# First modulation on column groups of TensorE with its loads in the operands' tiles, and modulation shares moved out of an output projection

## The chip, the cores and the metric

The kernel runs on one core of one Trainium2 chip. The metric is the device time of one execution in microseconds. Three runs of the kernel before took 1596.87 to 1600.23 us, median 1598.62.

## What is computed

Two residual blocks on 256 latent tokens and 256 context tokens of width 1024, in float32. Each block modulates, applies a SwiGLU feed-forward (hidden 2816), modulates, applies a mixer (a short convolution in block 0, grouped-query attention with 8 heads in block 1), modulates, and applies a second feed-forward:

```python
mod  = (silu(c) @ mod_w[i] + mod_b[i]).reshape(3, 3, D)       # shift, scale, gate, three times
modc = (silu(c_ctx) @ mod_w[i] + mod_b[i]).reshape(3, 3, D)
modulate(t, g, shift, scale) = rms(t) * g * (1 + scale) + shift
lat += 0.5 * mod[0, 2]  * swiglu(modulate(lat, g0, mod[0, 0], mod[0, 1]), w13, w2)
cx  += 0.5 * modc[0, 2] * swiglu(modulate(cx, g0, modc[0, 0], modc[0, 1]), w13, w2)
# mixer with mod[1], second feed-forward with mod[2]; in block 1 the context stops after the mixer's keys and values
```

The modulation is a product of one vector (two vectors: c and c_ctx) with a matrix of 1024 x 9216 per block.

## The kernel before, in words

Activations lie transposed: 8 tiles of 128 channels by 512 tokens (latent and context side by side). Every matrix product is done three times (`mm3`, lines 113 to 118): weight and activation are each split into a high part (`wh`, `hh`) and a low part (`wl`, `hl`), and high x high, high x low and low x high are added in PSUM. `split` (lines 91 to 93) makes the high part on ScalarE and the low part on VectorE. Weights arrive in `wr` tiles of 128x2048 (three buffers, `load_raw`, line 88, SP's queue).

The work is written with a tile framework that orders the instructions of each engine by readiness and priority, and sets the waits. A tile is allocated from a pool of a fixed number of buffers; an instruction that needs a new tile waits until an old one is free.

A feed-forward works in three parts of its 22 hidden tiles (8, 7, 7). For each hidden tile it loads W (gate and up halves) and does the products `pg` and `pu`; `w13_post` applies silu and product (`sg`, `gm`) and splits the result (`gh`, `gl`). After each part `project` multiplies by w2 (`py`) and adds into x (`finish`, line 440). In the first feed-forward the first eight hidden tiles are done with 48 plain matmuls of 512 columns each. Other parts of it use sums of quarter blocks of h (T1 to T4, `FirstBlocks.sums`, lines 353 to 373) in order to need fewer products.

The modulation is spread over the kernel. The part that the first norm needs (channels 0 and 1: shift B00 and scale A00) is cut into eight pieces (channel, quarter), which I call shares. `mod_pe` (lines 736 to 755) computes one on TensorE: eight matmuls with `sccol` (128 x 2) as the weights over 256 columns, a copy of the row (line 746), and two small matmuls that turn the row into columns (line 748). `mod_dve` computes one on VectorE instead: a load from `modT` and four units of line 136 (`junk`), each the product of a 128x1024 half with the broadcast vector `scbc` and its sum. All later channels are such units. `tick(n)` says how many units are added to the program at a place, and `mod_ready` adds what is still missing where a channel is needed.

The start follows a hand-written list, `FIRST_STEPS` (lines 34 to 37): W is the load and split of one of the first three weights, P a share on TensorE, D a share on VectorE, S the broadcast of the vectors (`load_sc`), N the norm of a quarter of h (`norm_q`: A00, t, hh, hl, and a raw copy hr for the sums), M the matmuls of one weight with one quarter (12 of 512 columns). So "P11 P10 P00 N0" are three shares and then the first quarter of h. Before it come 36 warming matmuls (`idle`) and the sums of squares (lines 214 to 242: `sq`, `acc`, `ss`, `rs`, `ri`, `ris`). After it, `w13_post` of the three weights, and the sums T1 to T4 in the middle of the next hidden tile.

In block 1, `scores`, `turn` and `mix` work through the heads with `tick(0.5)` in the loop; then `project` with `wo` and 1.2 units a tile, then the last norm (`tail_norm(1, 2, ...)`, which needs channels 6 and 7 of block 1) and the last feed-forward.

Of the kernel before, what the change touches and what calls it, by code (L numbers as in the profile page):

```python
# [9 lines left out]
F32 = mybir.dt.float32  # L10
# [3 lines left out]
ALU = mybir.AluOpType  # L14
# [12 lines left out]
KVH = 2  # L27
EPS = 1e-6
WARM = 36

FIRST_STEPS = (
    "W0 P11 P10 P00 N0 P01 N1 P12 W1 S M00 M10 M01 M11 D02 N2 M02 D13 W2 D03 M12 M20 M21 N3 "
    "M03 M22 M13 M23"
)


# [1 line left out]
def hybrid_kernel(ctx: ExitStack, tc: tile.TileContext, a: dict, out: bass.AP):  # L40
# [13 lines left out]
    def nm(s):  # L54
        uid[0] += 1
        return f"{s}{uid[0]}"
# [4 lines left out]
    def psmall(s="pq"):  # L61
        return pss.tile([P, T2], F32, tag="sm", name=nm(s))
# [15 lines left out]
    nc.vector.memset(ones, 1.0)  # L78
    eps_t = const.tile([P, 1], F32, name="eps_t", tag="eps_t")
    nc.vector.memset(eps_t, EPS)  # L80
# [92 lines left out]
    def tick(n):  # L173

        owed[0] += n
        while (jobs or units) and owed[0] >= 1:
            owed[0] -= 1
            next_unit()
# [44 lines left out]
                else:  # L223
                    accs[s, "last"] = part

    def rms_inv(s, parts):

        pq = psmall("ss")
        for i in range(2):
            for n, t in enumerate(parts):  # L230
                nc.tensor.matmul(
                    pq[:, S + i : S + i + 1], t[:, i * P : i * P + P], ones[:, 0:1],
                    start=(n == 0), stop=(n == len(parts) - 1),
                )
# [5 lines left out]
        nc.vector.reciprocal(ri, rs)  # L240
        for i in range(2):
            nc.tensor.matmul(
                pq[:, i * P : i * P + P], ri[:, i : i + 1].to_broadcast([P, P]), ident,
                start=True, stop=True,
            )
        return pq[:, :S]

    def scaled(s, k, A, ri):
        t = tp.tile([P, S], F32, name=nm("t"), tag="t", bufs=3)
        nc.vector.scalar_tensor_tensor(  # L250
            out=t, in0=x[:, k, s * S : s * S + S], scalar=A[:, k, s : s + 1], in1=ri,
            op0=ALU.mult, op1=ALU.mult,
        )
        return t

    def norm_k(s, k, h, A, B, ri, keep=None):
        hh, hl = pick(h, k, s * S, s * S + S)
        t = scaled(s, k, A, ri)
        b = B[:, k, s : s + 1]
        nc.scalar.activation(out=hh, in_=t, func=AF.Identity, bias=b)  # L260
        nc.vector.scalar_tensor_tensor(
            out=hl, in0=t, scalar=b, in1=hh.bitcast(F32), op0=ALU.add, op1=ALU.subtract
        )
        if keep is not None:
            nc.scalar.activation(out=keep, in_=t, func=AF.Identity, bias=b)

    def hot(s, dt=F32R):
        return hop.tile([P, 1024], dt, name=nm(s), tag="hop")
# [336 lines left out]
    def ffn(l, b, h, tot, gate, tail, gs=(), ev=1.5):  # L605
        gs = list(gs)
        i0 = 0
        for t, n in enumerate(THIRDS):
            between = ()
            if tot == T2:  # L610
# [22 lines left out]
                for i in range(len(gs), n):  # L633
                    if t == 0 and not heads and i in AS_IS[l, b]:
                        w = load_w(a["w13"][l, b, i])
                        pp = psum("pg"), psum("pu")
                        if prev:
                            prev.seven()
                        w13_mm(pp, w, h, range(4), 0, T2)
                        if prev:  # L640
                            gs.append(new_pair("g"))
                            prev.four(gs[-1])
                            prev = None
                        w13_mm(pp, w, h, range(4, KT), 0, T2)
                        gs.append(new_pair("g"))
                        w13_post(pp, gs[-1], 0, T2)
                        if "T1" not in h.t:
                            h.sums()
                        else:
                            tick(5)  # L650
# [61 lines left out]

    h = Plain()
    h32 = {}
    idle = psmall("idle")


    for _ in range(WARM):
        nc.tensor.matmul(idle[:, :P], ones, ones, start=True, stop=True)
    for k in range(KT):  # L720
        square_add(k, 0, T2)
    ris = []
    for s in range(2):
        ris.append(tp.tile([P, S], F32, name=nm("ris"), tag=f"ris{s}", bufs=1))
        nc.scalar.copy(ris[s], rms_inv(s, (accs[s], accs[s, "last"])))
# [7 lines left out]
    def both(t):  # L733
        return t.unsqueeze(2).to_broadcast([P, 2, 2])

    def mod_pe(ch, q):

        raw = load_raw(a["mod0"][ch, q])
        pr = psmall("pr")
        for k in range(KT):  # L740
            nc.tensor.matmul(
                pr[:2, :S], sccol[:, k, :], raw[:, k * S : k * S + S],
                start=(k == 0), stop=(k == KT - 1),
            )
        row = tp.tile([P, S], F32, name=nm("row"), tag="t", bufs=3)
        nc.scalar.copy(row[:2, :], pr[:2, :S])
        for j in range(2):
            nc.tensor.matmul(
                pr[:, S + 2 * j : S + 2 * j + 2], row[:2, j * P : j * P + P], ident[:2, :2],
                start=True, stop=True,  # L750
            )
        k2 = slice(2 * q, 2 * q + 2)
        nc.vector.tensor_tensor(
            out=(A00 if ch else B00)[:, k2, :],
            in0=pr[:, S : S + 4].rearrange("p (k v) -> p k v", v=2),
            in1=both(sb1[:, k2] if ch else modb[:, 0, k2]),
            op=ALU.add,
        )

    def norm_q(q):  # L760
        k2 = slice(2 * q, 2 * q + 2)
        nc.vector.tensor_tensor(
            out=A00[:, k2, :], in0=A00[:, k2, :], in1=both(normg[:, 0, 0, k2]), op=ALU.mult
        )
        for k in range(2 * q, 2 * q + 2):
            for s in range(2):
                if (q, s) not in h32:
                    h32[q, s] = gp.tile([P, T2], F32, name=nm("hr"), tag="gl" if s else "gh")
                norm_k(s, k, h, A00, B00, ris[s], h32[q, s][:, (k % 2) * S : (k % 2) * S + S])

    pps = [(psum("pg"), psum("pu")) for _ in range(3)]

    def mod_dve(ch, q):
        mod_job(0, ch, q)
        if ch:
            k2 = slice(2 * q, 2 * q + 2)
            nc.vector.tensor_scalar(
                out=A00[:, k2, :], in0=modv[0, 1][:, k2, :], scalar1=1.0, scalar2=None,
                op0=ALU.add,
            )  # L780

    ws, gs0 = {}, []

# [5 lines left out]
    def first_w(i):  # L789
# [8 lines left out]

    steps = {
        "P": mod_pe,  # L800
        "D": mod_dve,
        "S": load_sc,
        "W": first_w,
        "N": norm_q,
        "M": lambda i, q: w13_mm(pps[i], ws[i], h, range(2 * q, 2 * q + 2), 0, T2),
    }
    for step in FIRST_STEPS.split():
        steps[step[0]](*(int(c) for c in step[1:]))
# [11 lines left out]


    hn = Plain()
    ffn(0, 0, h, T2, lazy_gate(0, 0), tail_norm(0, 1, hn), gs0)
    h = hn

    zs = []
# [256 lines left out]
    pns, pts = {0: scores(0)}, {}  # L1083
    v_proj(2)
    v_proj(3)
    tick(1)
# [21 lines left out]
def _layout(inp):  # L1108
# [53 lines left out]
    sign = np.where(np.arange(P) % 64 < 32, -1.0, 1.0).astype(np.float32)  # L1162
    d["sinT"] = np.sin(ang).T * sign[:, None]
    d["ident"] = np.eye(P, dtype=np.float32)
    return {k: np.ascontiguousarray(v) for k, v in d.items()}


# [17 lines left out]
```

## Time and profile before

| what | value |
|---|---|
| median of three runs | 1598.62 us |
| profiled execution | 1600.64 us |
| its span, first to last instruction | 1598.9 us |
| mean granted TensorE clock | 0.993 |
| TensorE busy | 1575.3 us |
| VectorE busy | 1317.5 us |
| ScalarE busy | 719.0 us |
| moved from memory | 244.77 MB, 154 GB/s over the span |

PE is TensorE, PEld its weight loads, DVE VectorE, ACT ScalarE, SP the engine whose queue issues most transfers. A row of the timeline has the start in us, the duration, engine, line, operation, output and inputs, shape and count; in brackets the idle time ahead of it and what ended that. A row of the windows has, for a stretch of time, its length and then the busy time of PE, PEld, DVE, ACT and POOL with their instructions in brackets, then the granted clock, the busy share of the DMA engines and GB/s. A matmul's duration reaches past the start of the next, since they are pipelined: its cost in a stream is the distance between starts.

### The profile page before, as it was taken

The page shows a single profiled execution, that of the slowest core. Times are in us where ns is not written, and L with a number is a line of the kernel's source. Part 1 is how long each engine was busy: PE and PEld are TensorE (multiplying, and loading weights), DVE is VectorE, ACT ScalarE, POOL GpSimd, SP SyncE. Part 2 cuts the span into 40 slices and gives each one's busy share as a digit, 9 for nine tenths or more (in the row PEclk, how much of TensorE's full clock was granted, in tenths as well). Part 3 has the DMA queues.
Part 4 walks back from the last instruction along what each step waited for, and adds up shares of the span by engine and source line. Part 5 has one row for each costly group of instructions (what it writes and reads, how often), then busy time and mean ns, then how long its engine had stood idle before and what let it go on. Part 6 is the DMA issues. An engine that isn't in the chain of part 4 may idle for free.

```text
span 1598.9 us, 25657 instructions
## 1 busy us (share of the span) xinstructions
PE 1575.3 (99%) x10590; PEld 1450.4 (91%) x10590; DVE 1317.5 (82%) x2005; ACT 719.0 (45%) x1100; POOL 30.3 (2%) x20
## 2 busy tenths in 40 slices
PE   9999999999999999999999999999999999899999
PEld 5788998998888899989899899889899898899999
DVE  3998788889998879798798899898797789875554
ACT  4622452544322356435345376245255456454443
POOL 0000000000000000000000000000000005100000
PEclk9999999999999999999999999999999999999999
DMA  8555225324555512352342423452432454665452
GB/s 289 195 198 202 103 97 181 106 99 179 181 209 192 181 60 100 139 178 100 126 158 96 169 93 106 154 197 103 166 123 106 181 185 165 210 241 185 168 200 104
DMA packets 38278, 248.79 MB, mean 156 GB/s; under 512 B 5136, under 2 KB 6928, under 8 KB 12304
## 3 DMA queue, kind: packets, MB, share of 16 engines
q1 hardware_dynamic: 35712, 245.38, 43.8%
q10 hardware_dynamic: 2448, 1.76, 0.4%
q8 instruction: 83, 1.36, 0.3%
q14 instruction: 35, 0.29, 0.1%
HBM read 244.77 MB, written 1.05 MB: 154 GB/s over the span
## 4 chain that ended last, share of the span: by engine, by line
PE 90%; DVE 6%; ACT 2%; DMA 1%; issue 1%; POOL 0%; ACTq 0%; DVEq 0%; POOLq 0%
PE py L117 9%; PE py L116 9%; PE py L118 9%; PE p L118 6%; PE p L117 6%; PE p L116 6%; PE q L118 5%; PE q L116 5%; PE q L117 5%; PE pg L116 3%; PE pg L118 2%; DVE junk L136 2%; PE pg L117 2%; PE pu L118 2%; PE pu L117 2%; PE pu L116 2%
## 5 line engine op out<-in xcount | busy, mean ns | idle before, releaser
L92 ACT ACTIVATE wh<-wr 128x1024 fp32r<-128x1024 f32 (+2 forms) x276 | 276.7, 1014 | 371.6 <-PE py L117 118.0
L93 DVE TENSOR_TENSOR wl<-wr,wh 128x1024 fp32r<-128x1024 f32 (+2 forms) x276 | 320.7, 1168 | 90.2 <-ACT wh L92 89.6
L136 DVE CUSTOM_DVE_ANT_0 junk<-wr,scbc,modb 128x1024 bf16<-128x1024 f32 x236 | 302.4, 1281 | 29.5 <-DMA wr<-in_modT 26.8
L116 PE MATMUL py<-gh,wh 128*128 128x512 f32 (+1 forms) x746 | 263.2, 353 | 0.0
L117 PE MATMUL py<-gl,wh 128*128 128x512 f32 (+1 forms) x746 | 262.9, 352 | 0.0
L118 PE MATMUL py<-gh,wl 128*128 128x512 f32 (+1 forms) x746 | 262.9, 352 | 0.0
L118 PEld LDWEIGHTS py<-gh,wl 128*128 128x128 f32 x746 | 141.1, 189 | 19.1
L93 DVE TENSOR_TENSOR wl<-ws,wh 128x1024 fp32r<-128x1024 f32 x108 | 131.8, 1224 | 32.2 <-ACT wh L92 32.0
L116 PEld LDWEIGHTS py<-gh,wh 128*128 128x128 f32 x746 | 141.2, 189 | 18.5
L117 PEld LDWEIGHTS py<-gl,wh 128*128 128x128 f32 x746 | 141.2, 189 | 18.1
L92 ACT ACTIVATE wh<-ws 128x1024 fp32r<-128x1024 f32 x108 | 113.6, 1058 | 71.7 <-PE p L117 38.2
L118 PE MATMUL p<-th,wl 128*128 128x256 f32 x432 | 122.3, 283 | 0.0
L117 PE MATMUL p<-tl,wh 128*128 128x256 f32 x432 | 122.2, 283 | 0.0
L116 PE MATMUL p<-th,wh 128*128 128x256 f32 x432 | 122.2, 283 | 0.0
L440 DVE SCALAR_TENSOR_TENSOR x<-py,G,x 128x256 f32<-128x256 f32 x168 | 74.1, 479 | 24.9 <-PE py L118 24.9
L116 PE MATMUL q<-bh,wh 128*128 128x256 f32 x320 | 90.6, 283 | 0.0
L117 PE MATMUL q<-bl,wh 128*128 128x256 f32 x320 | 90.6, 283 | 0.0
L118 PE MATMUL q<-bh,wl 128*128 128x256 f32 x320 | 90.6, 283 | 0.0
L116 PEld LDWEIGHTS p<-th,wh 128*128 128x128 f32 x432 | 82.9, 192 | 0.3
L117 PEld LDWEIGHTS p<-tl,wh 128*128 128x128 f32 x432 | 82.9, 192 | 0.3
L118 PEld LDWEIGHTS p<-th,wl 128*128 128x128 f32 x432 | 82.9, 192 | 0.0
L116 PE MATMUL pg<-hh,wh 128*128 128x256 f32 (+1 forms) x240 | 75.8, 316 | 4.1 <-ACT hh L260 4.1
(236 smaller groups left out, 4054.6 us busy)
## 6 DMA issues: line engine op xcount, KB each, us to landing
wr<-in_w SPq DMA_DIRECT2D x88, 1024.0 KB, 4.9
wr<-in_modT SPq DMA_DIRECT2D x67, 1024.0 KB, 4.9
wr<-in_w2b SPq DMA_DIRECT2D x32, 896.0 KB, 4.6
wr<-in_w2a SPq DMA_DIRECT2D x16, 1024.0 KB, 5.0
wr<-in_cw_cx SPq DMA_DIRECT2D x8, 1024.0 KB, 4.9
wr<-in_mod SPq DMA_DIRECT2D x5, 1024.0 KB, 4.8
wr<-in_cw_b SPq DMA_DIRECT2D x4, 1024.0 KB, 5.0
wr<-in_cw_out SPq DMA_DIRECT2D x4, 1024.0 KB, 4.9
```

Of the source, the lines that this page charges most:

```text
L92: nc.scalar.activation(out=hi, in_=src, func=AF.Copy)
L93: nc.vector.tensor_tensor(out=lo, in0=src, in1=hi.bitcast(F32), op=ALU.subtract)
L116: nc.tensor.matmul(ps, wh, mh, start=first, stop=False, **kw)
L117: nc.tensor.matmul(ps, wh, ml, start=False, stop=False, **kw)
L118: nc.tensor.matmul(ps, wl, mh, start=False, stop=last, **kw)
L136: nc.vector.tensor_tensor_reduce(out=junk, in0=raw[:, j * D : j * D + D], in1=scbc[:, v, :], scale=1.0, scalar=modb[:, l, col : col + 1], ...
L440: nc.vector.scalar_tensor_tensor(out=x[:, m, s * S : s * S + S], in0=ps[:, o : o + S], scalar=g[:, m, s : s + 1], in1=x[:, m, s * S : s * ...
```

## The change

The list of first steps is rewritten. All eight shares go through TensorE. A share's raw data is loaded as two 128x1024 tiles from the pool of the operands' tiles (`hop`), not as one `wr` tile. `sccol` is widened to 32 columns (two filled, the others zero); the eight matmuls of a share write four groups of 32 partitions (`tile_position`), each group taking two of the eight, and the small matmuls that turn the row also add the four groups, with a constant `rowsum`. The turn is a step of its own (T), so that two shares can be computed ahead of two turns; F is eight filling matmuls; H makes the raw copies of a quarter, formerly inside N. TensorE's order in this stretch is fixed as written (`manual_schedule`); the vectors for VectorE's units are loaded where the scheduler has room (S is last in the list). The sums T1 to T4 come right after the first three weights.

Units: six after the first steps, five in each of the next five hidden tiles, 1.8 instead of 1.5 a tile in the first feed-forward's projections, two instead of one and 0.75 instead of 0.5 in attention, none in the projection with `wo`.

```diff
 FIRST_STEPS = (
-    "W0 P11 P10 P00 N0 P01 N1 P12 W1 S M00 M10 M01 M11 D02 N2 M02 D13 W2 D03 M12 M20 M21 N3 "
-    "M03 M22 M13 M23"
+    "P10 P00 T10 T00 N0 F W0 M00 W1 P11 P01 T11 T01 N1 H0 M10 W2 M01 P12 H1 M11 P02 T12 T02 "
+    "N2 M20 H2 M21 P13 P03 T13 T03 N3 M02 M12 M22 H3 M03 M13 M23 S"
 )
-    sccol = const.tile([P, KT, 2], F32, name="sccol", tag="sccol")
-    nc.scalar.activation(out=sccol, in_=ccol, func=AF.Silu)
+    sccol = const.tile([P, KT, 32], F32, name="sccol", tag="sccol")
+    nc.vector.memset(sccol, 0.0)
+    nc.scalar.activation(out=sccol[:, :, :2], in_=ccol, func=AF.Silu)
+
+    rowsum = cload("rowsum", [P, 2])
...
     def mod_pe(ch, q):
-        raw = load_raw(a["mod0"][ch, q])
-        pr = psmall("pr")
+        raws = []
+        for i in range(2):
+            raws.append(hot("pm", F32))
+            nc.sync.dma_start(raws[i], a["mod0"][ch, q, :, i * 1024 : i * 1024 + 1024])
+        pr = psum("pr") if (ch, q) == (1, 0) else psmall("pr")
         for k in range(KT):
+            g = 32 * (k % 4)
+            o = k % 4 * S
             nc.tensor.matmul(
-                pr[:2, :S], sccol[:, k, :], raw[:, k * S : k * S + S],
-                start=(k == 0), stop=(k == KT - 1),
+                pr[g : g + 32, :S], sccol[:, k, :], raws[k // 4][:, o : o + S],
+                start=(k < 4), stop=(k >= 4), tile_position=(0, g),
             )
-        row = tp.tile([P, S], F32, name=nm("row"), tag="t", bufs=3)
-        nc.scalar.copy(row[:2, :], pr[:2, :S])
+        row = tp.tile([P, T2], F32, name=nm("row"), tag="gm", bufs=3)
+        nc.scalar.copy(row[:, :S], pr[:, :S])
+        rows[ch, q] = pr, row
+
+    def mod_turn(ch, q):
+        pr, row = rows[ch, q]
         for j in range(2):
             nc.tensor.matmul(
-                pr[:, S + 2 * j : S + 2 * j + 2], row[:2, j * P : j * P + P], ident[:2, :2],
+                pr[:, S + 2 * j : S + 2 * j + 2], row[:, j * P : j * P + P], rowsum,
                 start=True, stop=True,
             )
...
+    with tc.manual_schedule(engines={mybir.EngineType.PE}):
+        fill(WARM)
+        sums = [rms_sum(s, (accs[s], accs[s, "last"])) for s in range(2)]
+        for step in FIRST_STEPS.split():
+            if step == "P00":
+                for s in range(2):
+                    ris.append(tp.tile([P, S], F32, name=nm("ris"), tag=f"ris{s}", bufs=1))
+                    nc.scalar.copy(ris[s], rms_all(*sums[s]))
+            steps[step[0]](*(int(c) for c in step[1:]))
...
         w13_post(pps[i], gs0[i], 0, T2)
+    h.sums()
+    tick(6)
...
-    ffn(0, 0, h, T2, lazy_gate(0, 0), tail_norm(0, 1, hn), gs0)
+    ffn(0, 0, h, T2, lazy_gate(0, 0), tail_norm(0, 1, hn), gs0, 1.8)
...
-        tick(0.5)
+        tick(0.75)
...
-        by_pairs("wo"), lambda k, c0, c1: aos[k], KT, lazy_gate(1, 1), tail_norm(1, 2, hn), S, 0, 1.2,
+        by_pairs("wo"), lambda k, c0, c1: aos[k], KT, lazy_gate(1, 1), tail_norm(1, 2, hn), S, 0, 0,
```

More of the change, by code (lines that the diff above doesn't have):

```diff
@@ L254, in scaled, with norm_k @@
         return t
[L256 removed]
+    def norm_k(s, k, h, A, B, ri, t=None):
         hh, hl = pick(h, k, s * S, s * S + S)
[L258 removed]
+        t = scaled(s, k, A, ri, t)
         b = B[:, k, s : s + 1]
@@ L263, in norm_k @@
         )
-        if keep is not None:
-            nc.scalar.activation(out=keep, in_=t, func=AF.Identity, bias=b)
+        return t
     def hot(s, dt=F32R):
@@ L646, in ffn @@
                         w13_post(pp, gs[-1], 0, T2)
[L647 to L650, printed above, removed]
+                        tick(5)
                         continue
@@ L714, in hybrid_kernel, with fill @@
     h32 = {}
-    idle = psmall("idle")
-    for _ in range(WARM):
-        nc.tensor.matmul(idle[:, :P], ones, ones, start=True, stop=True)
+    idle = psum("idle")
+    def fill(n):
+        for _ in range(n):
+            nc.tensor.matmul(idle[:, :P], ones, ones, start=True, stop=True)
     for k in range(KT):
         square_add(k, 0, T2)
[L722 to L725, printed above, removed]
     A00 = const.tile([P, KT, 2], F32, name="A00", tag="A00")
@@ L766, in norm_q, with copy_q, first_mm @@
             for s in range(2):
[L767 to L780, printed above, removed]
+                t = None
+                if k % 2:
+                    t = tp.tile([P, T2], F32, name=nm("t"), tag="sg", bufs=3)[:, :S]
+                ts[k, s] = norm_k(s, k, h, A00, B00, ris[s], t)
+    def copy_q(q):
+        for s in range(2):
+            h32[q, s] = gp.tile([P, T2], F32, name=nm("hr"), tag="gl" if s else "gh")
+            for k in range(2 * q, 2 * q + 2):
+                nc.scalar.activation(
+                    out=h32[q, s][:, (k % 2) * S : (k % 2) * S + S], in_=ts[k, s],
+                    func=AF.Identity, bias=B00[:, k, s : s + 1],
+                )
+    pps = {}
+    ris, ts = [], {}
+    def first_mm(i, q):
+        if q == 0:
+            pps[i] = psum("pg"), psum("pu")
+        w13_mm(pps[i], ws[i], h, range(2 * q, 2 * q + 2), 0, T2)
     ws, gs0 = {}, []
@@ L804, in hybrid_kernel @@
         "N": norm_q,
-        "M": lambda i, q: w13_mm(pps[i], ws[i], h, range(2 * q, 2 * q + 2), 0, T2),
+        "M": first_mm,
     }
-    for step in FIRST_STEPS.split():
-        steps[step[0]](*(int(c) for c in step[1:]))
+    with tc.manual_schedule(engines={mybir.EngineType.PE}):
[3 more added lines that the diff above has]
+            if step == "P00":
+                for s in range(2):
+                    ris.append(tp.tile([P, S], F32, name=nm("ris"), tag=f"ris{s}", bufs=1))
+                    nc.scalar.copy(ris[s], rms_all(*sums[s]))
+            steps[step[0]](*(int(c) for c in step[1:]))
     done[0, 0] = done[0, 1] = 16
@@ L1164, in _layout @@
     d["ident"] = np.eye(P, dtype=np.float32)
+    d["rowsum"] = (np.arange(P)[:, None] % 32 == np.arange(2)).astype(np.float32)
     return {k: np.ascontiguousarray(v) for k, v in d.items()}
```

19 lines of the change are left out of this document (14 added, 5 removed).

## The prediction

> **What bounds the kernel now.** I read the page first (shares of engines, then the chain that ended last), then windows over the first 130 us, then the timeline of each engine there.
>
> ```profile
> span 1598.9 us, 25657 instructions
> ...
> PE 1575.3 (99%) x10590; PEld 1450.4 (91%) x10590; DVE 1317.5 (82%) x2005; ACT 719.0 (45%) x1100; POOL 30.3 (2%) x20
> ...
> PE 90%; DVE 6%; ACT 2%; DMA 1%; issue 1%; POOL 0%; ACTq 0%; DVEq 0%; POOLq 0%
> ```
>
> The chain is 90% TensorE, so an edit pays if it starts the dense stream of matmuls earlier or closes one of its holes. The first projection matmul (py) is my milestone: ahead of it, both kernels have the same 384 matmuls of the gate and up products (eight blocks of 48).
>
> ```profile
> 39.38 0.50 PE L116 MATMUL pg<-hh,wh 128*128 128x512 f32 x1
> 67.76 0.50 PE L116 MATMUL pg<-hh,wh 128*128 128x512 f32 x1 [2.82 <-ACT hh L260]
> 130.46 0.39 PE L116 MATMUL py<-gh,wh 128*128 128x512 f32 x1
> 39.38:64.94 25.56, 25.55 (x113) 20.50 (x112) 24.16 (x48) 13.27 (x26) 0.00 (x0) 1.00 0.60 215
> 67.76:130.46 62.70, 62.70 (x276) 51.90 (x277) 59.42 (x89) 25.42 (x38) 0.00 (x0) 1.00 0.57 201
> ```
>
> The third column of a window row is TensorE. From 67.76 it is full: 62.70/276 = 0.227 us per matmul, 2.72 us for a step M of 12, 10.9 us for a block. The stream starts at 39.38 and loses 2.82 us waiting for h. What fills the time before 39.38 are the shares of the first modulation:
>
> ```profile
> 12.63 0.36 PE L231 MATMUL ss<-ones,sq 128*128 128x1 f32 x2
> 12.87 1.38 PE L242 MATMUL ss<-ident,ri 128*128 128x128 f32 x8
> 16.89 1.44 PE L741 MATMUL pr<-wr,sccol 128*2 128x256 f32 x3 [2.64 <-ACT wh L92]
> 28.02 0.60 PE L748 MATMUL pr<-ident,row 2*128 2x2 f32 x4
> 28.55 3.62 PE L741 MATMUL pr<-wr,sccol 128*2 128x256 f32 x16
> 31.34 0.36 ACT L746 COPY row<-pr 2x256 f32<-2x256 f32 x1 [3.71 <-PE pr L741]
> ```
>
> A share is eight matmuls in 16 passes over 3.62 us: 0.44 us a matmul, 0.22 us a pass. Four and a part of the fifth stand before the first gate matmul, and the first waits behind W0's load.
>
> **The change part by part: the start.** All eight shares now go through TensorE, each with its matmuls spread over four groups of 32 columns; their loads have tiles of their own, and the first two are ahead of W0 in SP's queue. No M waits for more than two shares. Three things could set the new start: transfers, the shares' passes, VectorE.
>
> Transfers:
>
> ```profile
> 0.00:10.00 10.00, 8.97 (x62) 8.97 (x63) 3.83 (x15) 5.14 (x9) 0.19 (x4) 1.00 0.86 274
> 10.00:16.00 6.00, 4.25 (x36) 3.91 (x35) 2.65 (x7) 4.81 (x10) 0.00 (x0) 0.95 0.99 401
> 16.00:22.00 6.00, 5.11 (x13) 1.54 (x14) 1.29 (x2) 0.77 (x2) 0.00 (x0) 0.50 0.78 269
> 34.00:46.00 12.00, 12.00 (x57) 7.34 (x56) 10.11 (x25) 11.54 (x23) 0.00 (x0) 1.00 0.85 316
> ```
>
> 2.74 MB move in the first 10 us; with the queue full, 401 GB/s. A share or a W is 1.05 MB, 2.6 us. Since SP no longer waits for one of three buffers before a share, I keep the queue full and count in its new order: P10 12, P00 14, W0 17, W1 20, P11 22, P01 25, W2 27.5, first half of scbc, P12 31, P02 34, second half, two modT, P13 43, P03 46. At 316 GB/s instead, the 36 us after 10 become 45 and P03 lands at 55.
>
> The shares' price is the open one. No row shows a matmul on a group of columns. From below: four at once, 3.54/4 = 0.9 us a share. From above: none overlap, 3.54 (the row). I take 2.0: the row shows two passes per matmul; the second needs the same columns as the first, so only the second pass of one can run beside the first of the next, which leaves one pass of spacing per matmul, 8 x 0.22 + 0.22. The Trainium skill, TensorE: Matmul & The Clock Gate, Part 3, says that matmuls start and end strictly in program order; that fits this count, and no run here shows it for column groups. The same section gives 2.38 times for three column groups; by that figure a share would cost about 1.5 us and the time would be 2 to 3 us under my forecast.
>
> Other durations:
>
> ```profile
> 1.03 10.28 PE L719 MATMUL idle<-ones 128*128 128x128 f32 x72 [1.03 <-DVE eps_t L80]
> 15.10 0.63 ACT L725 COPY ris<-ss 128x256 f32<-128x256 f32 x2
> 33.00 0.51 ACT L260 ACTIVATE hh<-t,mod 128x256 fp32r<-128x256 f32 x1 [1.30 <-DVE mod L753]
> 41.11 1.14 ACT L92 ACTIVATE wh<-wr 128x512 fp32r<-128x512 f32 x2
> 44.85 1.27 DVE L250 SCALAR_TENSOR_TENSOR t<-x,A,ris 128x256 f32<-128x256 f32 x3
> 43.05 1.89 DVE L93 TENSOR_TENSOR wl<-wr,wh 128x512 fp32r<-128x512 f32 x3
> 49.08 1.28 DVE L136 CUSTOM_DVE_ANT_0 junk<-wr,scbc,modb 128x1024 bf16<-128x1024 f32 x1
> 50.29 0.48 DVE L261 SCALAR_TENSOR_TENSOR hl<-t,mod,hh 128x256 fp32r<-128x256 f32 x1
> 74.66 1.22 DVE L93 TENSOR_TENSOR wl<-wr,wh 128x1024 fp32r<-128x1024 f32 x1
> ```
>
> TensorE in the written order: the sums end at 13.0 (12.63 + 0.36), P10 to 15.0, broadcasts 1.4 to 16.4, P00 to 18.4, row copy and turn 1.0 to 19.4. ScalarE then makes three hh and one raw copy (0.4 each) and two pieces of W0 (0.57 each): M00 starts at 22.4 and ends at 25.7, 0.6 of it waiting for wl. The eight fills (0.29 us each, 2.3) lie in those 3.0 us and cost nothing; if h came sooner they would cost up to 2.3. Then P11, P01 to 29.7, copy and turns 1.0, M10, M01 to 36.1, P12, M11, P02 to 42.8, turns to 43.8, M20, M21 to 49.3, P13, P03 to 53.3, turns to 54.3, and the last six steps (16.3) to 70.7. P03 landed at 46 is hidden behind M21; at 55 it costs 4.
>
> VectorE: N2 follows the turns of 43.8 and ends near 46.4. Its order then has eight units (junk, 1.2 each from one start to the next), three sums of 128x512 (0.6), N3 (3.5): 61.3, just before M03 needs it at 62.5. Eleven pieces for T1 to T4 bring 68.0, and gm, wl, gl, gm, wl of the fourth block 72.1. That block's third matmul needs the last wl; it could run at 71.2, so 0.9 is lost. Milestone: 70.7 + 0.9 + five blocks (54.4) = 126.1, against 130.46: **4.4 us gained**. Behind it VectorE has 31 units (6 and five times 5) to spread over 54 us, but its list for each next block ends 3 us or more before TensorE wants it, so I add nothing.
>
> Moved at no cost, with the cover: the raw copies (H) leave the path of hh and lie on ScalarE beside M steps; three shares' bytes replace those of three modT; rowsum's load takes ScalarE's queue half a microsecond before the silu, while x is still landing; the memset of sccol is over before silu needs it. Fixed order on TensorE: behind a waiting share everything waits, which the sum contains.
>
> **Units moved later on.** Twelve units vanish from VectorE at the start; 6.6 more (22 x 0.3) fall in the first FFN's projections, 8 us of VectorE.
>
> ```profile
> 130.00:175.00 45.00, 45.00 (x204) 37.44 (x203) 36.98 (x57) 12.51 (x14) 0.00 (x0) 1.00 0.47 164
> 175.00:400.00 225.00, 224.80 (x1607) 212.59 (x1607) 189.14 (x277) 106.32 (x162) 0.00 (x0) 1.00 0.36 127
> ```
>
> VectorE (fifth column) has 8 of 45 and 36 of 225 us free: nothing taken, up to 8 if cover failed. In the output projection (wo) the units now stop before its last tiles. Before, they stand on the path:
>
> ```profile
> 1396.66 0.28 PE L118 MATMUL py<-a,wl 128*128 128x256 f32 x1
> 1396.93 1.28 DVE L136 CUSTOM_DVE_ANT_0 junk<-wr,scbc,modb 128x1024 bf16<-128x1024 f32 x1 [1.46 <-DMA wr<-in_modT]
> 1398.48 0.48 DVE L440 SCALAR_TENSOR_TENSOR x<-py,mod,x 128x256 f32<-128x256 f32 x1
> 1399.46 0.38 PE L231 MATMUL ss<-ones,sq 128*128 128x1 f32 x2 [0.46 <-ACT sq L214]
> 1400.71 1.27 DVE L136 CUSTOM_DVE_ANT_0 junk<-wr,scbc,modb 128x1024 bf16<-128x1024 f32 x1
> 1400.85 0.88 PE L242 MATMUL ss<-ident,ri 128*128 128x128 f32 x4 [0.55 <-DVE ri L240]
> ```
>
> VectorE waits for a transfer with the last x and acc behind it. Freed, x starts when py ends (1397.0) instead of 1398.48, so 1.5 us; the second unit delays the norm by 0.2 more beyond 1401.73. **1.7 us gained**; what is late next is the norm's own chain. Attention gets 16 units instead of the 18 that I count in the lists of VectorE's instructions: no cost taken, within a unit or two either way.
>
> **Sum.** 4.4 + 1.7 = 6.1 us. The profiled execution took 1600.64 (its span 1598.9 and 1.7 around it), so 1594.5 by its own time; the median of the three runs is 2.0 below it, so 1592.5 is forecast.
>
> **Rivals.**
> Fully overlapped groups: 0.9 us a share. Then transfers bound: P03 lands at 46, M20 and M21 are over at 44.4, P03 ends at 47 to 48, the M steps at 65.4; VectorE (N2 ends 41.5, plus the same 25.7) holds the fourth block to 67.2, milestone 121.2. Gain 9.3 + 1.7: 1587.6. The Trainium skill, TensorEngine Tiling (Array Packing), Theoretical Speedup, promises up to four times for at most 32 columns; nothing here shows it, and the two passes per matmul in the row speak against it.
>
> Groups do not overlap at all: 3.54 us a share on a TensorE that is the bound. All eight then stand on the path, 8 x 1.54 = 12.3 us more, VectorE's 0.9 hidden: M steps end at 83.0, milestone 137.4, 6.9 later than before, less 1.7: **1603.9, slower**. It decides from 6.1/8 = 0.76 us above my 2.0, that is at 2.8 us a share. For it: the row, and three shares more than before; against: the matmuls have disjoint columns.
>
> The change doesn't start earlier as it says: the granted clock halves again. The row 16 to 22 shows 0.50 after 2.64 us of idle TensorE. With P10 and P00 in such a stretch they cost 4 us more, 2 us gained remain: about 1596.5, same. With P10 landed at 12, TensorE goes from the sums straight into P10, so this is less likely; a slow queue (316 GB/s) ends at the same time.
>
> **Chances.** Forecast 0.45 (1590 to 1595), full overlap 0.25, no overlap 0.18, clock or queue 0.12. A measurement tells about 0.2%, 3.2 us, from no change. Faster by over that: forecast and full overlap, 0.70; within: most of the fourth case, 0.10; slower: no overlap and the rest, 0.20. Range 1585 (full overlap with a little more saved in attention) to 1604 (no overlap).
>
> **What would show it.** The first gate matmul near 22 and the first py near 126; a share's 16 passes within 2 us; TensorE at 54 not waiting for P03's transfer; after the wo projection x starting within 0.3 us of py's end. Wrong if a share takes over 2.8 us, if TensorE sits behind a share whose load is late, or if VectorE's eight units delay N3 past M03.

## The result, and the profile after

The changed kernel took 1595.53 us (median of 17 runs, 1593.18 to 1599.21), the kernel before on the same chips 1598.11 us (median of 17, 1595.08 to 1600.65). The ratio is 0.9984 with a 95% interval of 0.9977 to 0.9991: about 2.6 us faster, a gain that the interval separates from nothing, but within the 0.2% that the prediction called the same. 6.1 us were forecast. The profiled execution of the changed kernel took its median, 1595.53 (span 1593.7 and 1.8 around it); that of the kernel before had taken 1600.64, 2.5 more than its own median here.

The page of the changed kernel: TensorE busy 6.5 us less, VectorE's part of the chain that ended last 4% where it was 6%.

```profile
span 1593.7 us, 25820 instructions
...
PE 1568.8 (98%) x10666; PEld 1449.7 (91%) x10666; DVE 1303.3 (82%) x1984; ACT 721.1 (45%) x1103; POOL 29.4 (2%) x20
...
PE 92%; DVE 4%; ACT 2%; DMA 1%; issue 0%; POOL 0%; ACTq 0%; DVEq 0%; POOLq 0%
```

The timeline of TensorE in the changed kernel's start (start, duration, what, and in brackets the wait ahead of it). L757 is a share's matmul (L741 before), L122 to L124 are the three products of a weight and operand pair (L116 to L118 before):

```profile
17.96 0.64 PE L757 MATMUL pr<-pm,sccol 128*32 128x256 f32 x8 [1.74 <-DMA pm<-in_mod]
...
23.09 0.50 PE L122 MATMUL pg<-hh,wh 128*128 128x512 f32 x1
...
28.31 0.64 PE L757 MATMUL pr<-pm,sccol 128*32 128x256 f32 x8 [0.74 <-DMA pm<-in_mod]
29.49 0.64 PE L757 MATMUL pr<-pm,sccol 128*32 128x256 f32 x8 [0.54 <-DMA pm<-in_mod]
...
37.11 1.07 PE L757 MATMUL pr<-pm,sccol 128*32 128x256 f32 x16
...
42.07 1.22 PE L769 MATMUL pr<-rowsum,row 128*128 128x2 f32 x8
...
48.80 1.93 PE L757 MATMUL pr<-pm,sccol 128*32 128x256 f32 x32
50.66 1.22 PE L769 MATMUL pr<-rowsum,row 128*128 128x2 f32 x8
...
69.77 0.50 PE L122 MATMUL pg<-hh,wh 128*128 128x512 f32 x1 [0.39 <-ACT wh L98]
73.20 0.50 PE L124 MATMUL pg<-hh,wl 128*128 128x512 f32 x1 [2.70 <-DVE wl L99]
...
128.90 0.39 PE L122 MATMUL py<-gh,wh 128*128 128x512 f32 x1
```

The first gate matmul comes 16.3 us earlier than in the kernel before (39.38), the first projection matmul py only 1.6 us earlier (130.46). The same 384 matmuls lie between them, so 14.7 us of the lead are given back on the way. Some 11 of these are the six shares and their turns that now stand behind the first gate matmul (26.4 to 31.1, 37.0 to 38.1, 41.0 to 43.2 and 48.7 to 51.7, with 1.3 us of waits among them); the prediction had them in its sum, and between its 22.4 and its 126.1 the lead shrinks by 12.6. What it had not counted on are the 0.7 us by which the first gate matmul comes later than forecast and 2.1 us behind it. The largest single hole is the last wait: TensorE stands at the fourth gate block for 2.70 us because VectorE has not made the low part of its weights. What VectorE and ScalarE did in the meantime (one timeline of each, put in order of time; L142 is a unit of a later modulation, L774 and L264 are the first steps of the last norm tile, N3):

```profile
46.42 1.27 DVE L142 CUSTOM_DVE_ANT_0 junk<-wr,scbc,modb 128x1024 bf16<-128x1024 f32 x1
...
57.04 0.16 DVE L774 TENSOR_TENSOR A<-pr,sb 128x4 f32<-128x4 f32 x1
...
57.31 1.28 DVE L142 CUSTOM_DVE_ANT_0 junk<-wr,scbc,modb 128x1024 bf16<-128x1024 f32 x1
58.51 1.27 DVE L264 SCALAR_TENSOR_TENSOR t<-x,A,ris 128x256 f32<-128x256 f32 x3
59.03 1.31 ACT L274 ACTIVATE hh<-t,mod 128x256 fp32r<-128x256 f32 x3 [7.80 <-DVE t L264]
...
66.59 2.49 DVE L99 TENSOR_TENSOR tl<-hr,th 128x512 fp32r<-128x512 f32 x4
...
71.93 1.22 DVE L99 TENSOR_TENSOR wl<-wr,wh 128x1024 fp32r<-128x1024 f32 x1
```

The turns that N3 needs are over on TensorE at 51.9. VectorE takes them up at 57.04, behind seven of its eight units, and the eighth still goes ahead of N3's first t. From 46.42 to 73.07 it is never idle for longer than 0.6 us, and the last thing in that row is the weight half that TensorE waits for. The windows of TensorE around the hole (length, busy time, granted clock, share of the DMA engines, GB/s) show what it cost beside the wait itself:

```profile
70.00:72.00 2.00, 0.50 (x2) 1.00 0.00 0
72.00:74.00 2.00, 0.80 (x3) 1.00 0.00 0
74.00:76.00 2.00, 2.00 (x6) 0.52 0.84 250
76.00:78.00 2.00, 2.00 (x7) 0.63 0.65 274
```

Right behind it the granted clock is halved from 74.1 to 77.5: six and seven matmuls fit in 2 us where nine do at full clock, some 1.6 us more. The clock is halved once before, from 19.5 to 22.9, behind the wait for the second half of P00; there it falls on the turns and the filling matmuls. Late in the kernel, in the output projection of the attention, the step that the units had blocked is free (timeline of all engines):

```profile
1392.83 0.28 PE L124 MATMUL py<-a,wl 128*128 128x256 f32 x1
1393.15 0.48 DVE L453 SCALAR_TENSOR_TENSOR x<-py,mod,x 128x256 f32<-128x256 f32 x1 [1.35 <-PE py L124]
```

x is started 0.04 us after the last product's end (1393.11); in the kernel before it was 1.54 us.

### The profile page after: what moved, and what is told of

The parts are those of the page before. It is cut to its first block, busy times and chain, and to the rows that moved or that the text cites. A ratio compares the mean times of both kernels' runs of the same rounds, so it can differ in the third digit from the quotient of the medians.

```text
span 1593.7 us, 25820 instructions
## 1 busy us (share of the span) xinstructions
PE 1568.8 (98%) x10666; PEld 1449.7 (91%) x10666; DVE 1303.3 (82%) x1984; ACT 721.1 (45%) x1103; POOL 29.4 (2%) x20
## 4 chain that ended last, share of the span: by engine, by line
PE 92%; DVE 4%; ACT 2%; DMA 1%; issue 0%; POOL 0%; ACTq 0%; DVEq 0%; POOLq 0%
PE py L123 10%; PE py L122 10%; PE py L124 10%; PE p L124 7%; PE p L123 7%; PE p L122 6%; PE q L122 5%; PE q L124 5%; PE q L123 5%; PE pg L122 2%; PE pg L124 2%; PE pg L123 2%; PE pu L124 2%; PE pu L123 2%; PE pu L122 2%; PE pv L122 1%
## 5 line engine op out<-in xcount | busy, mean ns | idle before, releaser
L142 DVE CUSTOM_DVE_ANT_0 junk<-wr,scbc,modb 128x1024 bf16<-128x1024 f32 x224 | 286.9, 1281 | 31.8 <-DMA wr<-in_modT 29.0
L122 PE MATMUL py<-gh,wh 128*128 128x512 f32 (+1 forms) x746 | 263.3, 353 | 0.0
L124 PE MATMUL py<-gh,wl 128*128 128x512 f32 (+1 forms) x746 | 262.7, 352 | 0.0
L124 PEld LDWEIGHTS py<-gh,wl 128*128 128x128 f32 x746 | 141.1, 189 | 19.0
L122 PEld LDWEIGHTS py<-gh,wh 128*128 128x128 f32 x746 | 141.2, 189 | 18.6
L124 PE MATMUL p<-th,wl 128*128 128x256 f32 x432 | 122.3, 283 | 0.0
L122 PE MATMUL p<-th,wh 128*128 128x256 f32 x432 | 122.2, 283 | 0.0
L453 DVE SCALAR_TENSOR_TENSOR x<-py,G,x 128x256 f32<-128x256 f32 x168 | 73.9, 477 | 23.1 <-PE py L124 23.1
L122 PE MATMUL q<-bh,wh 128*128 128x256 f32 x320 | 90.6, 283 | 0.0
L124 PE MATMUL q<-bh,wl 128*128 128x256 f32 x320 | 90.6, 283 | 0.0
L122 PEld LDWEIGHTS p<-th,wh 128*128 128x128 f32 x432 | 82.9, 192 | 0.3
L124 PEld LDWEIGHTS p<-th,wl 128*128 128x128 f32 x432 | 82.9, 192 | 0.0
L124 PE MATMUL pg<-hh,wl 128*128 128x256 f32 (+1 forms) x240 | 75.5, 315 | 2.8 <-DVE wl L99 2.7
```

Of the source, the lines that this page charges most:

```text
L122: nc.tensor.matmul(ps, wh, mh, start=first, stop=False, **kw)
L124: nc.tensor.matmul(ps, wl, mh, start=False, stop=last, **kw)
L142: nc.vector.tensor_tensor_reduce(out=junk, in0=raw[:, j * D : j * D + D], in1=scbc[:, v, :], scale=1.0, scalar=modb[:, l, col : col + 1], ...
L453: nc.vector.scalar_tensor_tensor(out=x[:, m, s * S : s * S + S], in0=ps[:, o : o + S], scalar=g[:, m, s : s + 1], in1=x[:, m, s * S : s * ...
```

## The experiments

**The theory.** TensorE is no longer what holds the start back. VectorE's list is: its units of later modulations stand ahead of the last norm tile, so the early start ends in a wait, and the wait in a halved clock. **Rivals**: TensorE's fixed list and the transfers it waits for set the start; or the shares themselves are still dear. Besides: what the late part (units moved out of the output projection) is worth.

All profiled executions in one table, us, with the median of 4 to 17 runs. "First gate" and "py" are the starts of the first gate and the first projection matmul, "middle" is the time from that py to the first py of the third group in the second layer's first feed-forward, "rest" from there to the end of the span. Ratios are to the kernel before, with 95% intervals.

| kernel | first gate | py | middle | rest | median | ratio |
|---|---|---|---|---|---|---|
| before | 39.4 | 130.5 | 1103.2 | 365.2 | 1598.11 | |
| changed | 23.1 | 128.9 | 1102.4 | 362.4 | 1595.53 | 0.9984 (0.9977 to 0.9991) |
| a_one_chain | 27.3 | 142.3 | 1101.3 | 362.4 | 1607.11 | 1.0051 (1.0038 to 1.0065) |
| f_groups_in_before | 27.7 | 126.1 | 1102.2 | 363.1 | 1596.02 | 0.9985 (0.9975 to 0.9996) |
| e_units_later | 22.1 | 121.2 | 1108.2 | 362.1 | 1593.43 | 0.9976 (0.9965 to 0.9987) |
| e2_units_spread | 22.0 | 124.5 | 1101.8 | 360.9 | 1587.62 | 0.9928 (0.9915 to 0.9941) |
| c_wo_as_before | 21.6 | 128.8 | 1102.6 | 364.5 | 1596.30 | 0.9994 (0.9983 to 1.0004) |
| d_late_alone | 36.3 | 129.0 | 1103.4 | 362.4 | 1597.42 | 1.0002 (0.9993 to 1.0012) |
| g_groups_and_late | 28.8 | 127.8 | 1103.5 | 362.3 | 1594.90 | 0.9978 (0.9969 to 0.9987) |
| e3_more_fill | 22.1 | 122.7 | 1100.4 | 360.9 | 1587.41 | 0.9934 (0.9920 to 0.9948) |
| e4_m10_first | 22.6 | 123.6 | 1102.1 | 363.3 | 1590.09 | 0.9947 (0.9933 to 0.9961) |
| h_no_fill | 21.6 | 121.5 | 1101.9 | 362.4 | 1588.55 | 0.9939 (0.9926 to 0.9952) |

The columns of times come from one execution each, and they scatter: kernels whose edits differ only behind the first py have it 1.5 us apart (before and d), 1.7 (f and g), 0.1 (changed and c, with first gate matmuls 1.5 apart) and 3.3 (e and e2).

### What a share costs: a_one_chain and f_groups_in_before

a_one_chain is the changed kernel with the groups taken out:

```diff
-            g = 32 * (k % 4)
+            g = 0
...
-                start=(k < 4), stop=(k >= 4), tile_position=(0, g),
+                start=(k == 0), stop=(k == KT - 1),
```

> The changed kernel with each share as one chain of eight products in one group of 32 columns (only rows 0 to 31 copied and added up). Theory (the four groups overlap, 1.07 us a share against 3.5): 16 passes near 3.5 us again, eight shares some 20 us longer, of which the transfers that are waited for hide 3 and the vanished wait for VectorE with its half clock gives back 4.3: first output-projection matmul near 141, whole near 1608, ratio 1.006. Rival (groups do not matter here, passes are cheap in any form): 16 passes near 1.1 us, ratio 0.998 as the changed kernel. Rival by the prediction's 2.0 us a share: 8 us slower than the changed kernel, ratio 1.003.

Measured: 1.0051, first py at 142.28. The timeline of its TensorE:

```profile
20.08 3.64 PE L757 MATMUL pr<-pm,sccol 128*32 128x256 f32 x16
...
63.30 7.09 PE L757 MATMUL pr<-pm,sccol 128*32 128x256 f32 x32
```

The same 16 passes take 3.64 us in one group of columns and 1.07 in four: 3.4 times less. Without the groups the changed kernel would have been slower than the one before. The theory's numbers held (141, 1608). The prediction's 2.0 us a share had this kernel at 1.003; that is outside the interval.

f_groups_in_before is the kernel before with the groups, and nothing else of the change:

```diff
-                pr[:2, :S], sccol[:, k, :], raw[:, k * S : k * S + S],
-                start=(k == 0), stop=(k == KT - 1),
+                pr[g : g + 32, :S], sccol[:, k, :], raw[:, k * S : k * S + S],
+                start=(k < 4), stop=(k >= 4), tile_position=(0, g),
```

> The kernel before with only the four column groups of the modulation's shares (one 256-column product of k 0 to 7 in four groups of 32 columns, rows added up by the turn's second operand); tiles, order and units as before. Theory (a share falls from 3.6 to about 1.1 us, but VectorE's order, whose low weights of the fourth block end at 76, sets the time): first gate matmul up to 10 us earlier than 39.4, first output-projection matmul at most 2.5 earlier than 130.5, ratio 0.998 to 1.000. Rival (TensorE's own work sets the start): the first output-projection matmul 8 us or more earlier, ratio 0.995 or less.

Its TensorE, by the timeline:

```profile
32.13 1.07 PE L745 MATMUL pr<-wr,sccol 128*32 128x256 f32 x16
...
61.99 0.80 PE L119 MATMUL pg<-hh,wh 128*128 128x512 f32 x1 [3.05 <-ACT hh L263]
...
126.05 0.39 PE L119 MATMUL py<-gh,wh 128*128 128x512 f32 x1
```

The first gate matmul is 11.7 us earlier than in the kernel before, the first py 4.4 (2.9 against d_late_alone, which has the same front as the kernel before); the wait for the last norm tile stays (3.05, it was 2.82). Ratio 0.9985: the groups alone bring as much as the whole change. The py gain is over the 2.5 that the theory allowed, by either count, and under the 8 of its rival. The new order of loads and of TensorE added nothing measurable to it as it stood; the next two runs show that the units are in its way.

### Who holds the start: e_units_later and e2_units_spread

e_units_later takes the units out of VectorE's way and gives them back later:

```diff
     h.sums()
-    tick(6)
...
-                        tick(5)
+                        tick(7 if i > 4 else 0)
...
-    ffn(0, 0, h, T2, lazy_gate(0, 0), tail_norm(0, 1, hn), gs0, 1.8)
+    ffn(0, 0, h, T2, lazy_gate(0, 0), tail_norm(0, 1, hn), gs0, 2.25)
```

> The changed kernel with no share of a later modulation issued before the sixth gate block (six after the third block and five after each of the fourth and fifth go; seven after each of the last three instead of five, and 2.25 for 1.8 after each output tile make them up), so that VectorE has no such unit ahead of the last first-norm tile. Theory (VectorE's order eats the early start): the wait of 2.7 us for the fourth block's low weights at 73 and the half clock behind it (about 1.6) go, the first output-projection matmul comes near 125 instead of 128.9, the whole near 1591.5, ratio to the kernel before near 0.996. Rival 1 (the fixed order of TensorE and the late transfers set the start): first output-projection matmul stays at 128.9, whole 1595.5, ratio 0.998. Rival 2 (the next one in line, ScalarE's high weights, takes the wait's place): half of it, near 127 and 1593.5.

Its VectorE and, below the dots, its TensorE:

```profile
50.35 0.48 DVE L264 SCALAR_TENSOR_TENSOR t<-x,A,ris 128x256 f32<-128x256 f32 x1
...
61.72 1.23 DVE L99 TENSOR_TENSOR wl<-wr,wh 128x1024 fp32r<-128x1024 f32 x1 [0.72 <-ACT wh L98]
...
63.46 2.35 DVE L99 TENSOR_TENSOR wl<-wr,wh 128x1024 fp32r<-128x1024 f32 x2
...
69.99 1.28 DVE L142 CUSTOM_DVE_ANT_0 junk<-wr,scbc,modb 128x1024 bf16<-128x1024 f32 x1
...
121.18 0.39 PE L122 MATMUL py<-gh,wh 128*128 128x512 f32 x1
...
278.01 0.39 PE L122 MATMUL q<-th,wh 128*128 128x256 f32 x1 [1.58 <-ACT wh L98]
279.27 0.39 PE L124 MATMUL q<-th,wl 128*128 128x256 f32 x1 [0.53 <-DVE wl L99]
```

N3 starts at 50.35 rather than 58.51, the second half of the fourth block's low weights is there by 65.8 rather than 73.2, and py starts at 121.2, 7.7 us earlier than in the changed kernel and more than the 4 expected; e2_units_spread below, with the same front, has 124.5, so 4.4 to 7.7 us. c_wo_as_before, with the changed kernel's front, has its wait of 2.70 us again, and none of the five kernels without the units has a wait of over 0.5 us there: the rival (TensorE's list and the transfers) is out. Of the 7.7, 1.0 is the first gate matmul's, 2.7 the wait, 1.6 the clock behind it; the rest (2.4) is small gaps: raw tiles (0.5 us of waits for 1.3 behind the first gate matmul), the fourth block's high weights (0.4), and N3's tiles, whose lateness stretches M03 by 1.0. By the two ratios the whole gained only some 1.3 us on the changed kernel, and their intervals overlap. The middle grew by 5.8: with 2.25 units after each output tile the second group's weights came late (the last two rows; 4.7 us more from the second group's first py to the third's), with a half clock behind the wait again (windows of TensorE):

```profile
275.00:280.00 5.00, 2.89 (x22) 1.00 0.03 10
280.00:285.00 5.00, 5.00 (x32) 0.66 0.60 210
```

e2_units_spread puts these ten units where VectorE has room:

```diff
-    ffn(0, 0, h, T2, lazy_gate(0, 0), tail_norm(0, 1, hn), gs0, 2.25)
+    ffn(0, 0, h, T2, lazy_gate(0, 0), tail_norm(0, 1, hn), gs0, 1.8)
...
-    ffn(0, 1, h, T2, lazy_gate(0, 2), tail_norm(1, 0, hn), (), 1.7)
+    ffn(0, 1, h, T2, lazy_gate(0, 2), tail_norm(1, 0, hn), (), 1.9)
...
-    ffn(1, 0, h, T2, lazy_gate(1, 0), tail_norm(1, 1, hn), (), 1.6)
+    ffn(1, 0, h, T2, lazy_gate(1, 0), tail_norm(1, 1, hn), (), 1.8)
```

> As e_units_later, but the ten units that its larger share per output tile put into the first feed-forward's projections go into the next two feed-forwards instead (1.8 after each tile of the first as in the changed kernel, then 1.9 for 1.7 and 1.8 for 1.6). Theory (the 4.6 us that e_units_later lost between its second and third groups of output tiles were VectorE's, from those ten units: waits of 2.4 us for the pair's weights and a clock of 0.96): first output-projection matmul near 121, the third group near 341 instead of 345.8, whole 4.6 us under e_units_later, near 1588.5, ratio to the kernel before near 0.994 to 0.995. Rival (the gain is lost again wherever the ten units go): ratio 0.9976 as e_units_later.

Measured: 1587.62 us, ratio 0.9928 (0.9915 to 0.9941), the middle back at 1101.8. That is a version that beats both kernels: 8 us under the changed one by the medians, 9 by the ratios, with the same work. Its py came only at 124.5, with the front that gave 121.2 in e_units_later. The timeline of TensorE shows the waits in it; the longest, 1.46 us, is in both:

```profile
21.96 0.50 PE L122 MATMUL pg<-hh,wh 128*128 128x512 f32 x1 [1.46 <-ACT wh L98]
...
27.34 0.64 PE L757 MATMUL pr<-pm,sccol 128*32 128x256 f32 x8 [0.73 <-DMA pm<-in_mod]
28.52 0.64 PE L757 MATMUL pr<-pm,sccol 128*32 128x256 f32 x8 [0.54 <-DMA pm<-in_mod]
```

and its windows a half clock behind them that e_units_later does not have, from 29.6 to 36.4, which costs some 3.4 us:

```profile
28.00:30.00 2.00, 1.48 (x14) 0.91 0.97 395
30.00:32.00 2.00, 2.00 (x7) 0.50 1.02 406
...
34.00:36.00 2.00, 2.00 (x6) 0.50 1.04 406
```

### The late part: c_wo_as_before, d_late_alone, g_groups_and_late

c undoes it in the changed kernel, d does it alone, g does it with the groups:

```diff
-    tick(2)
+    tick(1)
...
-        tick(0.75)
+        tick(0.5)
...
-        by_pairs("wo"), lambda k, c0, c1: aos[k], KT, lazy_gate(1, 1), tail_norm(1, 2, hn), S, 0, 0,
+        by_pairs("wo"), lambda k, c0, c1: aos[k], KT, lazy_gate(1, 1), tail_norm(1, 2, hn), S, 0, 1.2,
```

(as in c; the other way round in d and g).

> The changed kernel with the second layer's units as before: one and 0.5 per head in the attention, 1.2 after each tile of the output projection. Theory (the late move is worth what the milestones show, 1.2 in the attention and 1.4 behind the output projection): 2.6 us slower than the changed kernel, near 1598, ratio to the kernel before near 1.000. By the prediction's own term (1.7): 1597.2, ratio 0.9995. Rival (these milestones were only scatter between two executions): 1595.5, ratio 0.998.

> The kernel before with only the late part of the change: two and 0.75 units per head in the attention, none in the output projection. Theory: 2.6 us faster than the kernel before, near 1595.5, ratio 0.9984. By the prediction's term (1.7): ratio 0.9989. Rival (scatter): ratio 1.000.

> The kernel before with the column groups of the shares and the late part of the change, and nothing else of it. Theory (late move worth 2 us by the profiled executions: 362.1 to 362.5 us from the last first-layer-width output tiles to the end with it, 363.1 to 365.2 without): 2 us under f_groups_in_before, near 1594, ratio near 0.9972. Rival (the late move is worth nothing, as d_late_alone's ratio of 1.0002 says): ratio near 0.9985.

By the medians' ratios the late part is worth 1.0 thousandth (c against the changed kernel), 0.7 (g against f) and -0.2 (d against before): 1.6, 1.1 and -0.3 us, each with an interval of some 1.5 to 2.2 us either way. In the profiled executions "rest" is 365.2, 363.1 and 364.5 where the late part is missing (mean 364.3) and 360.9 to 363.3 in the nine where it is there (mean 362.1). So about 2 us by the profiles, and 0 to 2 by the times.

The profiles also say that this is not the step that the prediction freed. In c and f the units stand in the projection as before, and the last x is started 0.12 and 0.14 us after its last product all the same: the stall of 1.54 us is in the one execution of the kernel before and not in these. What goes with "rest" is the granted clock, which comes in half-clock periods of 3.4 us (last section). Apart from the one in which the execution ends, "rest" holds four of them in the kernel before (365.2), three in f, c and e4 (363.1, 364.5, 363.3), two in the changed kernel, a, d, g and h (362.3 to 362.4) and one in e, e2 and e3 (360.9 to 362.1). That the late move makes such periods rarer is not shown.

### The half clock in the front: e3_more_fill, e4_m10_first, h_no_fill

```diff
-FILL = 8
+FILL = 14
```

(e3; h has 0. e4 is e3 with the order "P11 M10 P01" instead of "P11 P01 ... M10".)

> e2_units_spread with 14 fill products ahead of the first gate matmul instead of 8, which run on through the 1.46 us that TensorE waits there for ScalarE's high weights. Theory (the half clock seen in the front, 29.1 to some 36 us in e2_units_spread, 18.9 to 23 in the changed kernel, 23.6 to 27 in c_wo_as_before and not at all in e_units_later, is set off by the gaps ahead of it, which add up to 2.7 us in e2_units_spread): no half clock in the front, first output-projection matmul near 121, 1 to 3 us under e2_units_spread, ratio near 0.992 to 0.991. Rival (the clock falls by itself, whatever the gaps): a half-clock stretch of 3 us or more in the front, ratio 0.9928.

> e3_more_fill with the second gate block's first products ahead of the second shift share, so that they lie in the wait for that share's transfer. Theory (what TensorE waits for the raw tiles, 1.7 us in e2_units_spread, is hidden by 12 matmuls): these waits fall under 0.5 us, first output-projection matmul 1 us earlier than e3_more_fill's, ratio near 0.991. Rival (the second block's weights come later than that share): the wait moves to the weights, ratio as e3_more_fill.

> e2_units_spread without the eight fill products between the first turns and the first gate matmul. Theory (gaps set off the half clock): a gap of some 3.4 us ahead of the first gate matmul, a half-clock stretch in the front behind it, first output-projection matmul at 124.5 or later. Rival (the fills do nothing): ratio 0.9928, and no half clock that the other front does not have.

Neither more fills nor none made a difference that can be told from e2's: 0.9934, 0.9939, 0.9928 with overlapping intervals. The wait that e3 was to cover went, and the half clock came all the same at 30.0 to 33.4, after 1.8 us of waits for raw tiles. h has a hole of 3.35 us and its half clock earlier, from 19.8 to 26.7, partly in time in which TensorE waits anyway:

```profile
18.00:20.00 2.00, 0.29 (x3) 0.96 1.05 428
20.00:22.00 2.00, 0.36 (x1) 0.50 0.99 406
22.00:24.00 2.00, 2.00 (x6) 0.50 1.02 413
```

Its py (121.5) is the earliest but one. e4 hid part of the waits for raw tiles (1.1 us left of 1.8) and got one of 1.4 for the second norm tile in their place; 0.9947 is no better than e3. The theories of e3 and e4 missed; that of h had the hole and the half clock right and py wrong. What the five fronts with VectorE out of the way show is py between 121.2 and 124.5, with the half clock absent, early or late, whichever hole was filled. Part of how the clock picks its place is in the last section.

## Why the prediction was right and wrong

- **Direction and range** held (1585 to 1604, faster), the size didn't: 2.6 us came of 6.1.
- **The price of a share (2.0 us) failed, to the good side.** It measured 1.07 undisturbed, 1.93 for two in a row, close to the 0.9 of the rival with full overlap. The argument behind 2.0, that the second pass of a matmul keeps the next group's first pass out, is refuted by these rows. The Trainium skill, TensorEngine Tiling (Array Packing), Theoretical Speedup, promises up to four times for up to 32 columns; the 3.4 measured here is near it.
- **The landings failed, to the bad side.** The second half of P00 was waited for until 17.96 (14 counted), those of P01 until 28.3 and 29.5 (25 counted): 3.0 us of waits. With shares at half the price this came out nearly even: first gate matmul at 23.09 for 22.4 predicted, the last shares at 48.80 without a wait.
- **VectorE's chain was sized almost rightly:** N2's end 46.4 (forecast 46.4), N3's end 62.4 (61.3), last weights 73.1 (72.1). But the prediction charged it 0.9 us, the difference to a TensorE that would want these weights at 71.2. TensorE wanted them at 70.5 and waited 2.70 us.
- **The step that failed is "so 0.9 is lost".** It counts the wait and not the clock behind it (1.6 us). From 73.20, when the fourth block's third matmul runs, 238 matmuls at 0.227 (54.0) and these 1.6 give 128.8, the py that was measured (128.90) where 126.1 was forecast: 1.0 of the 2.8 too much is VectorE's, 1.6 the clock, the rest rounding. VectorE being the bound, what the cheap shares saved on TensorE could not arrive. The prediction named the condition ("if VectorE's eight units delay N3 past M03") and gave it no chance of its own. It came true in part: M03 began at 60.03, N3 ended at 62.4, and M03 took 3.7 us where a step of 12 takes 2.7. In the rival with full overlap it let VectorE's list slide five us earlier with the shares; the turns that start N2 ended at 43.3 all the same, for 43.8 in the forecast, since the raw tiles came late, and N2 ended at 46.4 as forecast.
- **The start that the gain was counted from is one of several.** The 130.46 of the kernel before contains a half clock from 15.4 to 22.3 that another execution of the same front (d_late_alone) does not have. In its place d has a half clock behind its wait for the last norm tile, where the kernel before, with a wait of 2.82 us, has none. So its first gate matmul is 3.1 us earlier and its py 1.5. The windows of the kernel before, then rows of d_late_alone:

```profile
14.00:22.00 8.00, 5.36 (x16) 0.59 0.84 303
```

```profile
14.00:22.00 8.00, 7.01 (x36) 1.00 0.89 319
...
36.28 0.50 PE L116 MATMUL pg<-hh,wh 128*128 128x512 f32 x1
...
64.66 0.72 PE L116 MATMUL pg<-hh,wh 128*128 128x512 f32 x1 [2.75 <-ACT hh L260]
64.77:68.18 3.41, 3.41 (x9) 0.50 0.81 295
...
128.95 0.39 PE L116 MATMUL py<-gh,wh 128*128 128x512 f32 x1
```

  Against d's 128.95 the changed kernel's start gains nothing, one execution against one. The prediction had quoted the 0.50 of that stretch and priced it as a rival for the changed kernel, but subtracted the profile's 2.0 us above the median from the end as if they lay elsewhere.
- **The late part** (1.7): its size lies between 0 and 2 us, but its mechanism is not borne out. x starts 0.04 us after the last product as forecast, and within 0.14 also in c and f, without the late part; the 1.5 us were a stall of one execution. That the size comes out near the forecast by the profiles is luck. The middle was rightly left at nothing (1102.4 against 1103.2).
- **The rival that came nearest by its time** was "the clock halves again" (1596.5), at another place than it said. The stretch from 19.5 to 22.9 fell on turns and fills just behind the first shares: with it and the late load the first gate matmul came at 23.09, against 21.6 to 22.6 in the six others that start with column groups in this order. The one that cost 1.6 us stood behind VectorE's weights.

## What to carry to other kernels

When a stream of matmuls is started earlier, look on the engine that feeds it for work that was placed into its idle time: it doesn't move along, and what was a filler becomes the bound. Price a hole in TensorE's stream at its length and, if it is 2.7 us or more, some 1.6 us for the clock behind it: of the six such holes between 58 and 74 us here (2.70 to 3.05 us) five led to a half clock. Look for such a stretch in the profile that the gain is counted from, and don't take a difference of 1 to 3 us between two single profiles for an effect. Work taken off a path comes back where it is put: ten units of VectorE cost 4.7 us in one feed-forward and nothing measurable in the next two.

## What the runs showed of the hardware

- Eight 128x256 f32 matmuls with 32 columns of weights: 16 passes in 3.64 us in one column group, in 1.07 us over four. f32 operands, of which each matmul needs two passes, overlap as well across groups.
- The half clock comes in periods of 3.41 us. In all twelve profiles each half-clock stretch inside the span lasts one such period or a whole number of them (3.4 us in the changed kernel, 6.8 in e2_units_spread, 10.2 in f, 17.1 in g), and the stretches of one execution begin whole numbers of periods apart (19.45 and 74.06 in the changed kernel: 16 periods). So where the clock can change is fixed within an execution. Another execution has these places elsewhere: 29.62 in e2_units_spread and 280.04 in e_units_later, with the same front, are 73.4 periods apart.
- What a hole does depends on how much of one period it takes. Windows of one period at full clock, of the changed kernel (ahead of 74.06, with nearly all of the 2.70 us) and of the kernel before (whose 2.82 us lie across two periods):

```profile
70.65:74.06 3.41, 0.85 (x4) 1.00 0.00 0
```

```profile
63.22:66.64 3.42, 1.72 (x8) 1.00 0.84 321
66.64:70.05 3.41, 2.29 (x10) 1.00 0.63 199
```

  In the dense stream a half clock followed full-clock periods with 0.36 (g), 0.66 (d), 0.85, 0.89 (f), 1.33 (c) and 1.50 us (e_units_later, at 276.6) of busy TensorE, and none those with 1.72 and 2.29. Among the shares this does not hold: 2.15 us of busy time (e2_units_spread, 26.20 to 29.62) was followed by a half clock, and 1.88 (19.38 to 22.79, same execution, with the 1.46 us of waiting) was not. What else counts there is open.
- The Trainium skill, TensorE: Matmul & The Clock Gate, Part 1, has a free-running window of about 3.4 us that lowers the clock when idle. The periods of 3.41 us, fixed ahead of any hole, fit that window; that no whole window was idle, neither in e2_units_spread nor ahead of 74.06, doesn't fit the rule as it stands.
